# A two-layer decoder trunk: the tile pools of SBUF put at other places of a partition

## The chip, the core and the metric

The kernel runs on one core of a Trainium2 chip. The metric is the device time of that core in microseconds (us), from the first to the last instruction of one launch with what lies around it. Three runs of the kernel before took 659.36, 659.92 and 660.2 us; their median, 659.92 us, is the time before.

## The reference

A residual stream x of 256 tokens by 1024 columns, in fp32, goes through two layers, each a mixer and a gated feed-forward network (FFN), with an RMS norm ahead of each:

```python
for layer in range(2):
    h = rmsnorm(x, norm_mix[layer])
    if layer % 2 == 0:            # even: indexed sparse attention (8 heads, top 64 keys)
        y = h @ ev_w_in           #       beside differential attention (4 heads)
        mix = concat([dsa_mixer(...), diff_mixer(...)]) @ ev_w_out
    else:                         # odd: compressed, selected and window attention (16 heads)
        y = h @ od_w_in
        mix = nsa_mixer(...) @ od_w_out
    x = x + mix
    x = x + (silu(h2 @ w_gate) * (h2 @ w_up)) @ w_down     # h2 = rmsnorm(x, norm_ffn[layer]), 2816 wide
return rmsnorm(x, norm_final)
```

All weights are fp32 and each is used once, 107 MB in all.

## The kernel before

**Numbers.** To keep fp32 accuracy with TensorE's faster fp32r format, every weight tile and every activation is split into a high part (rounded to fp32r) and a low part (the rest). A product is then three matmuls: high by high, high by low, low by high. The helper `mm3` issues these three; its lines are L330, L331 and L332 of the profile. In the FFN's gate and up projections one matmul of 512 columns takes the high weight by both parts of the activation (L437), and one of 256 columns the low weight by the high part (L438).

**Weights.** `Weights` streams tiles of 128 partitions by 4096 bytes from HBM. `load` (L95) issues the DMA on SyncE's queue into one of four raw buffers (`w_raw`), now and then into the buffer of the norm's gain; `prepare` makes the high part on ScalarE (L110) into one of seven `w_hi` buffers and the low part on VectorE (L113) into one of seven `w_lo` buffers. Preparation runs six tiles ahead of use.

**Stages.** Per layer: input projection, attention, output projection, gate and up, down projection. In a projection into the mixer (`project`) the activation `aW` is the stationary operand (128 columns, loaded by LDWEIGHTS) and the weight is the moving operand of 512 columns or fewer, into `ps_in`. The output projection and the FFN's down projection are one function, `residual`: the stationary operand is the attention's output `aT` (`oT` in the code), or the FFN's hidden activation `hT_hi`/`hT_lo`; the moving operand is the weight, in two halves of 512 columns; four accumulators `ps_out` are used in turn. In gate and up the weight is stationary and `aW` moving, into `ps_g` and `ps_u`. Transposes through TensorE have the data as the stationary operand and an identity matrix, the first 128 columns of the constants `con`, as the moving one.

**Order.** A scheduling layer sets the order of each engine from data dependences, and semaphores between the engines; places marked with `keep_in_program_order` (`pin`) hold theirs. Buffers of one tag are used in rotation, so a write to a buffer waits for the readers of what was there.

**Where the buffers lie.** Each tile pool is a stretch of the 229,376 bytes of a partition. Within a pool the tiles follow each other in the order in which their tags first appear, each padded to a multiple of 32 bytes. Before, all pools grow from the low end: `base` (x, constants), `wpool` (raw, high and low weights), `acts` (small activations, and `aW` among them), and behind them the pool of the present stage (`even`, `ffn` or `odd`), which is given back when the stage ends.

Of the kernel before, what the change touches and what calls it, by code (L numbers as in the profile page):

```python
# [7 lines left out]
F32 = mybir.dt.float32  # L8
F32R = mybir.dt.float32r
# [7 lines left out]
T = 256  # L17
P = 128
NT = T // P
KD = D // P  # L20
# [11 lines left out]
WCOLS = 1024  # L32
# [6 lines left out]
def ff_kk(w):  # L39
    return WCOLS // w  # L40


def layer_tiles(chunks):
    tiles = in_tiles(chunks) + [(1, D)] * KD
    for w in FF_CHUNKS:
        tiles += [(ff_kk(w), w)] * (2 * KD // ff_kk(w))
    return tiles + [(1, D)] * KF
# [27 lines left out]
class Weights:  # L75


    def __init__(self, tc, pool, flats, specs, ahead, bufs, spare):
        self.tc, self.pool, self.ahead, self.bufs, self.spare = tc, pool, ahead, bufs, spare
        self.queue = []  # L80
        for flat, tiles in zip(flats, specs):
            off = 0
            for kk, w in tiles:
                n = kk * w
                self.queue.append((flat[off : off + P * n].rearrange("(p c) -> p c", p=P), kk, w))
                off += P * n
        self.raw = []
        self.ready = []
        self.used = 0

    def load(self, upto):
        while len(self.raw) < min(upto, len(self.queue)):
            src, kk, w = self.queue[len(self.raw)]
            raw = self.spare(len(self.raw)) or self.pool.tile([P, WCOLS], F32, tag="raw", bufs=self.bufs[0], name="w_raw")
            self.tc.keep_in_program_order(self.tc.nc.sync.dma_start(raw[:, : kk * w], src))  # L95
            self.raw.append(raw)

# [27 lines left out]
def trunk(tc, x, w0, w1, sm0, cw, vec, gcol, cst, out, dbg=None):  # L125
# [3 lines left out]
    from contextlib import ExitStack  # L129

    ctx = ExitStack()
    base = ctx.enter_context(tc.tile_pool(name="base", bufs=1))
    wpool = ctx.enter_context(tc.tile_pool(name="wpool", bufs=1))
    ap = ctx.enter_context(tc.tile_pool(name="acts", bufs=1))
    psum = ctx.enter_context(tc.tile_pool(name="psum", bufs=1, space=PSUM))

    def mm_bank(name):
        return psum.tile([P, 512], F32, tag="mm", bufs=4, name=name)

    def s_bank(name):  # L140
        return psum.tile([P, 512], F32, tag="s", bufs=2, name=name)

    def t_bank(name):
        return psum.tile([P, 512], F32, tag="tp", bufs=2, name=name)

    def nat(name):
        return ap.tile([P, 512], F32, tag="nat", bufs=4, name=name)


    tiles = [layer_tiles(EV_CHUNKS), layer_tiles(OD_CHUNKS)]  # L150
# [7 lines left out]
            return ap.tile([P, D], F32, tag="gain", bufs=1, name="w_raw")  # L158
        return None

    W = Weights(tc, wpool, [w0, w1], tiles, ahead=6, bufs=(4, 7), spare=spare)
    xs = [base.tile([P, D], F32, tag=f"x{t}", name=f"x{t}") for t in range(NT)]
    con = base.tile([P, C_END], F32, tag="con", name="con")
    small = base.tile([P, V_END - V_KV], F32, tag="small", name="small")
# [8 lines left out]
    def gain(off):  # L173
        new_gain(off)
        tc.keep_in_program_order(load_gain(off, nc.sync))
# [17 lines left out]
    def load_x(t, h):  # L193
        c = slice(512 * h, 512 * h + 512)
        pin(nc.sync.dma_start(xs[t][:, c], x[t * P : (t + 1) * P, c]))

    load_x(0, 0)
    W.load(1)
    load_x(1, 0)
    W.load(2)  # L200
    load_x(0, 1)
    load_x(1, 1)
    W.load(4)
    pin(nc.sync.dma_start(con[:, P:], cst[:, P:]))
# [10 lines left out]
    def evac(dst, src):  # L215
        A.activation(dst, src, AF.Copy)
# [10 lines left out]
    def small_tile(n, tag, bufs=4):  # L227
        return ap.tile([P, n], F32, tag=tag, bufs=bufs, name=tag)
# [4 lines left out]

    def new_wide():

        w = ap.tile([P, KD, 2, T], F32R, tag="aW", name="aW")
        return w, [[w[:, :, z, t * P : (t + 1) * P] for z in range(2)] for t in range(NT)]

    def split(hi, lo, src):
        A.activation(hi, src, AF.Copy)  # L240
        V.tensor_sub(lo, src, hi)  # L241
# [10 lines left out]
    class Norm:  # L252


        def __init__(self, goff):
            self.goff = goff
            self.wide, self.aT = new_wide()
            self.rs = [small_tile(1, "rs") for _ in range(NT)]
            self.last = None
            self.ms = [None] * NT  # L260
# [73 lines left out]
    def project(aT, w, nm=None):  # L334
# [4 lines left out]
        for g in range(n):  # L339
            wh, wl = W.next()  # L340
            for i in range(kk):
# [6 lines left out]
    def residual(act, nk, tail, nxt, rs=None, amid=None):  # L348
# [3 lines left out]
        def one(t, h, k, wt):  # L352
            c = slice(512 * h, 512 * h + 512)
            mm3(ps[t][h], act[t], k, wt[0][:, 0, c], wt[1][:, 0, c], k == 0, k == nk - 1)

        for k in range(nk - tail):
            wt = W.next()
            for t in range(NT):
                for h in range(2):
                    one(t, h, k, wt)  # L360
        last = [W.next(hold=tail) for _ in range(tail)]
        if amid:
# [39 lines left out]
    def ffn(nm, goff):  # L402
        wide, rs = nm.wide, nm.rs
        gain(goff)
        nxt = Final() if goff == V_FIN else Norm(goff)
        with tc.tile_pool(name="ffn", bufs=1, reuse_waits="tile") as fp:
            hh = fp.tile([P, KF, T], F32R, tag="hh", name="hT_hi")
            hl = fp.tile([P, KF, T], F32R, tag="hl", name="hT_lo")


            ones = fp.tile([P, P], F32, tag="ones", name="ones")
            G.memset(ones, 1.0)
            rB = fp.tile([P, T], F32, tag="rB", name="rB")

            def spread():
                dg = nat("dg")
                pb = t_bank("ps_r")
                for t in range(NT):
                    c = slice(t * P, (t + 1) * P)
                    V.tensor_scalar(dg[:, c], ident, rs[t], None, op0=ALU.mult)  # L420
                    TE.matmul(pb[:, c], ones, dg[:, c], start=True, stop=True)
                evac(rB, pb[:, :T])

            f0 = 0
            for w in FF_CHUNKS:
                kk = ff_kk(w)
                nf = w // P
                gp = [mm_bank("ps_g") for _ in range(nf)]
                up = [s_bank("ps_u") for _ in range(nf)]
                for dst in (gp, up):  # L430
                    for g in range(KD // kk):
                        wh, wl = W.next()
                        for i in range(kk):
                            k = g * kk + i
                            for f in range(nf):
                                c = slice(f * P, (f + 1) * P)
                                TE.matmul(dst[f], wh[:, i, c], wide[:, k].rearrange("p z q -> p (z q)"), start=k == 0, stop=False)  # L437
                                TE.matmul(dst[f][:, :T], wl[:, i, c], wide[:, k, 0], start=False, stop=k == KD - 1)  # L438
                        nm.finish()
                    if dst is gp and f0 == 0:  # L440
                        spread()
                for f in range(nf):
                    sg = fp.tile([P, T], F32, tag="sg", bufs=3, name="sg")
                    hn = fp.tile([P, T], F32, tag="hn", bufs=3, name="hn")
                    evac(sg, gp[f][:, T:])
                    V.tensor_add(sg, gp[f][:, :T], sg)
                    V.tensor_mul(sg, sg, rB)
                    A.activation(sg, sg, AF.Silu)
                    evac(hn, up[f][:, T:])
                    V.tensor_add(hn, up[f][:, :T], hn)  # L450
                    V.tensor_mul(hn, hn, sg)
                    split(hh[:, f0 + f], hl[:, f0 + f], hn)
                f0 += nf
            hT = [[z[:, :, t * P : (t + 1) * P] for z in (hh, hl)] for t in range(NT)]
            residual(hT, KF, 3, nxt, rs)
        return nxt


    def even_mixer(nm, goff):
        aT, rs = nm.aT, nm.rs  # L460
        with tc.tile_pool(name="even", bufs=1, reuse_waits="tile") as pool:

            def early(name):
                return pool.tile([P, D], F32, tag="aT", bufs=2 * NT, name=name)
# [248 lines left out]

    def odd_mixer(nm, goff):
        aT, rs = nm.aT, nm.rs
        with tc.tile_pool(name="odd", bufs=1, reuse_waits="tile") as pool:

            def early(name):
                return pool.tile([P, D], F32, tag="aT", bufs=2 * NT, name=name)
# [227 lines left out]
    for t in range(NT):  # L947
        for h in range(2):
            first.square(t, h)
    n = even_mixer(first, V_FFN0)  # L950
    n = ffn(n, V_MIX1)
    n = odd_mixer(n, V_FFN1)
    ffn(n, V_FIN)
    ctx.close()

# [129 lines left out]
```

## Time and profile before

| what | value |
|---|---|
| median of three runs | 659.92 us |
| span of the profiled execution | 658.3 us (no other time of that execution is listed; the median lies 1.6 us above the span) |
| TensorE matmul busy | 644.6 us (98%) |
| VectorE, ScalarE, GpSimd busy | 488.3, 396.6, 12.9 us (74%, 60%, 2%) |
| mean granted TensorE clock | 0.996 |
| DMA | 109.15 MB, 166 GB/s over the span |
| gate and up of the first layer, of the second | 139 to 263 us, 467 to 590 us |
| down projection of the first layer, of the second | 263 to 325 us, 590 to 651 us |

Times are from the start of the span. Busy shares are of the span. Matmuls are pipelined and the profile models their ends, so a matmul's listed duration is longer than the distance to the next; where it matters, distances between starts are read instead. The chain of waits follows the last instruction back to what released it, at each step.

### The profile page before, as it was taken

The page shows a single profiled execution, that of the slowest core. Times are in us where ns is not written, and L with a number is a line of the kernel's source. Part 1 is how long each engine was busy: PE and PEld are TensorE (multiplying, and loading weights), DVE is VectorE, ACT ScalarE, POOL GpSimd, SP SyncE. Part 2 cuts the span into 40 slices and gives each one's busy share as a digit, 9 for nine tenths or more (in the row PEclk, how much of TensorE's full clock was granted, in tenths as well). Part 3 has the DMA queues.
Part 4 walks back from the last instruction along what each step waited for, and adds up shares of the span by engine and source line. Part 5 has one row for each costly group of instructions (what it writes and reads, how often), then busy time and mean ns, then how long its engine had stood idle before and what let it go on. Part 6 is the DMA issues. An engine that isn't in the chain of part 4 may idle for free.

```text
span 658.3 us, 10005 instructions
## 1 busy us (share of the span) xinstructions
PE 644.6 (98%) x3512; PEld 535.8 (81%) x3512; DVE 488.3 (74%) x1115; ACT 396.6 (60%) x800; POOL 12.9 (2%) x26
## 2 busy tenths in 40 slices
PE   8999999999999999999999999999999999999995
PEld 5978888788888888888888877776888888888884
DVE  5999977758978787543579889796698787875424
ACT  6786758548755555433377599696586555554312
POOL 2000000000000000000000000000000000000000
PEclk8999999999999999999999999999999999999999
DMA  8844354038866666663098312420486666665501
GB/s 295 298 132 150 97 183 139 32 133 260 249 194 190 193 188 191 192 190 112 25 372 279 126 39 97 160 65 1 159 270 212 192 191 192 193 192 186 189 10 65
DMA packets 31729, 109.15 MB, mean 166 GB/s; under 512 B 3648, under 2 KB 3904, under 8 KB 31424
## 3 DMA queue, kind: packets, MB, share of 16 engines
q1 hardware_dynamic: 31104, 107.92, 51.2%
q8 instruction: 28, 0.46, 0.3%
q10 hardware_dynamic: 576, 0.59, 0.3%
q14 instruction: 21, 0.17, 0.1%
HBM read 107.46 MB, written 1.05 MB: 165 GB/s over the span
## 4 chain that ended last, share of the span: by engine, by line
PE 85%; ACT 5%; DVE 4%; DMA 3%; issue 2%; POOL 0%; SPq 0%; POOLq 0%; ACTq 0%
PE ps_u L437 12%; PE ps_g L437 11%; PE ps_out L330 7%; PE ps_out L332 7%; PE ps_out L331 7%; PE ps_u L438 6%; PE ps_g L438 6%; PE ps_in L330 5%; PE ps_in L331 5%; PE ps_in L332 5%; DMA w_raw<-in_w 3%; PE ps_o L934 2%; PE pt_p L918 2%; PE ps_s L899 2%; ACT w_hi L110 1%
## 5 line engine op out<-in xcount | busy, mean ns | idle before, releaser
L113 DVE TENSOR_TENSOR w_lo<-w_raw,w_hi 128x1024 fp32r<-128x1024 f32 (+5 forms) x200 | 234.9, 1182 | 95.1 <-ACT w_hi L110 92.9
L110 ACT ACTIVATE w_hi<-w_raw 128x1024 fp32r<-128x1024 f32 (+5 forms) x200 | 203.3, 1022 | 133.2 <-PE ps_out L332 59.6
L437 PE MATMUL ps_u<-aW,w_hi 128*128 128x512 f32 x352 | 123.4, 394 | 0.4 <-DVE hn L450 0.4
L437 PE MATMUL ps_g<-aW,w_hi 128*128 128x512 f32 x352 | 123.4, 394 | 0.3 <-DVE aW L241 0.3
L438 PE MATMUL ps_g<-aW,w_lo 128*128 128x256 f32 x352 | 97.6, 277 | 0.0
L438 PE MATMUL ps_u<-aW,w_lo 128*128 128x256 f32 x352 | 97.6, 277 | 0.0
L437 PEld LDWEIGHTS ps_g<-aW,w_hi 128*128 128x128 f32 x352 | 66.0, 187 | 16.2 <-DVE aW L241 0.9
L437 PEld LDWEIGHTS ps_u<-aW,w_hi 128*128 128x128 f32 x352 | 66.0, 188 | 15.9 <-DVE hn L450 0.7
L330 PE MATMUL ps_in<-w_hi,aW 128*128 128x512 f32 (+5 forms) x208 | 77.3, 372 | 0.6 <-ACT aW L240 0.6
L331 PE MATMUL ps_in<-w_lo,aW 128*128 128x512 f32 (+5 forms) x208 | 77.4, 372 | 0.1
L332 PE MATMUL ps_in<-w_hi,aW 128*128 128x512 f32 (+5 forms) x208 | 75.6, 364 | 0.0
L332 PE MATMUL ps_out<-w_hi,hT_lo 128*128 128x512 f32 x176 | 69.4, 395 | 0.0
L331 PE MATMUL ps_out<-w_lo,hT_hi 128*128 128x512 f32 x176 | 69.4, 395 | 0.0
L330 PE MATMUL ps_out<-w_hi,hT_hi 128*128 128x512 f32 x176 | 69.4, 395 | 0.0
L438 PEld LDWEIGHTS ps_g<-aW,w_lo 128*128 128x128 f32 x352 | 66.1, 188 | 0.0
L438 PEld LDWEIGHTS ps_u<-aW,w_lo 128*128 128x128 f32 x352 | 66.1, 188 | 0.0
L400 ACT ACTIVATE e<-e,bias 128x128 f32<-128x128 f32 (+1 forms) x96 | 42.4, 446 | 2.4 <-DVE bias L399 2.4
L330 PEld LDWEIGHTS ps_in<-w_hi,aW 128*128 128x128 f32 x208 | 39.5, 190 | 5.3 <-ACT aW L240 0.8
L331 PEld LDWEIGHTS ps_in<-w_lo,aW 128*128 128x128 f32 x208 | 39.5, 190 | 4.4 <-issue 0.5
L332 PEld LDWEIGHTS ps_in<-w_hi,aW 128*128 128x128 f32 x208 | 39.4, 189 | 4.4 <-issue 0.5
L332 PEld LDWEIGHTS ps_out<-w_hi,hT_lo 128*128 128x128 f32 x176 | 32.9, 187 | 8.1
L330 PEld LDWEIGHTS ps_out<-w_hi,hT_hi 128*128 128x128 f32 x176 | 32.9, 187 | 8.0
(225 smaller groups left out, 888.1 us busy)
## 6 DMA issues: line engine op xcount, KB each, us to landing
w_raw<-in_w SPq DMA_DIRECT2D x176, 512.0 KB, 4.3
w_raw<-in_w SPq DMA_DIRECT2D x8, 384.0 KB, 4.5
gain<-in_vec SPq DMA_DIRECT2D x4, 512.0 KB, 4.4
cw<-in_cw SPq DMA_DIRECT2D x2, 1024.0 KB, 7.7
w_raw<-in_w SPq DMA_DIRECT2D x4, 416.0 KB, 5.2
w_raw<-in_w SPq DMA_DIRECT2D x4, 328.0 KB, 5.2
w_raw<-in_w SPq DMA_DIRECT2D x4, 304.0 KB, 2.9
x<-in_x SPq DMA_DIRECT2D x4, 256.0 KB, 5.2
```

What stands on the lines that cost most here:

```text
L110: act = nc.scalar.activation(hi[:, :n], raw[:, :n], AF.Copy)
L113: nc.vector.tensor_sub(lo[:, :n], raw[:, :n], hi[:, :n])
L330: TE.matmul(ps, act[0][:, k], wh, start=start, stop=False)
L331: TE.matmul(ps, act[0][:, k], wl, start=False, stop=False)
L332: TE.matmul(ps, act[1][:, k], wh, start=False, stop=stop)
L400: A.activation(e, e, AF.Exp, scale=-1.0, bias=bias, accum_out=den)
L437: TE.matmul(dst[f], wh[:, i, c], wide[:, k].rearrange("p z q -> p (z q)"), start=k == 0, stop=False)
L438: TE.matmul(dst[f][:, :T], wl[:, i, c], wide[:, k, 0], start=False, stop=k == KD - 1)
L899: mmi = TE.matmul(sb[:, i], qS[t][:, h], kz[:, par, :, :ns], start=z == 0, stop=z == 1)
L918: TE.transpose(pt[:, i, b, st], e[:, i, b, st * P : (st + 1) * P], ident)
L934: pin(TE.matmul(ob[64 * par : 64 * par + 64], vv[:, st, c : c + 64], pTs[par][:, b, st].rearrange("p j c -> p (j c)"), start=False, stop=l ...
```

## The change

The pools are put on two sides. From the low end now grow `wpool` with the high and low weights only, a new pool `widep` with `aW` alone, and the stage's pool. From the high end grow `base`, a new pool `rpool` with the raw weights, and `acts`. No size, tag, rotation or instruction differs: each engine's list is the same in the same order, and every instruction waits for the same semaphore counts. The addresses in the built program, in bytes of a partition:

| buffer | bytes | start before | start now |
|---|---|---|---|
| x, two halves | 2 x 4096 | 16512 | 214752 |
| constants `con` | 4264 | 24704 | 222944 |
| `w_raw` | 4 x 4096 | 31104 | 198368 |
| `w_hi` | 7 x 4096 | 47488 | 16512 |
| `w_lo` | 7 x 4096 | 76160 | 45184 |
| `aW` | 16384 | 106880 | 73856 |
| `nat` (x times gain, rope and others) | 4 x 2048 | 123392 | 184608 |
| gain | 4096 | 131712 | 192928 |
| `hT_hi` | 22528 | 137152 | 90240 |
| `hT_lo` | 22528 | 159680 | 112768 |
| attention's output `aT`, even layer | 4 x 4096 | 137152 | 90240 |
| attention's output `aT`, odd layer | 4 x 4096 | 143040 | 96128 |

So TensorE's operands lie 31 to 47 thousand bytes lower, except the identity in `con`, x, and what is transposed out of `nat`, which lie higher.

```diff
 class Weights:
-    def __init__(self, tc, pool, flats, specs, ahead, bufs, spare):
-        self.tc, self.pool, self.ahead, self.bufs, self.spare = tc, pool, ahead, bufs, spare
+    def __init__(self, tc, pool, rpool, flats, specs, ahead, bufs, spare):
+        self.tc, self.pool, self.rpool, self.ahead, self.bufs, self.spare = tc, pool, rpool, ahead, bufs, spare
...
-            raw = self.spare(len(self.raw)) or self.pool.tile([P, WCOLS], F32, tag="raw", bufs=self.bufs[0], name="w_raw")
+            raw = self.spare(len(self.raw)) or self.rpool.tile([P, WCOLS], F32, tag="raw", bufs=self.bufs[0], name="w_raw")
...
-    base = ctx.enter_context(tc.tile_pool(name="base", bufs=1))
-    wpool = ctx.enter_context(tc.tile_pool(name="wpool", bufs=1))
-    ap = ctx.enter_context(tc.tile_pool(name="acts", bufs=1))
+    base = ctx.enter_context(tc.tile_pool(name="base", bufs=1, side="right"))
+    rpool = ctx.enter_context(tc.tile_pool(name="rpool", bufs=1, side="right"))
+    ap = ctx.enter_context(tc.tile_pool(name="acts", bufs=1, side="right"))
+    wpool = ctx.enter_context(tc.tile_pool(name="wpool", bufs=1, side="left"))
+    wide_pool = ctx.enter_context(tc.tile_pool(name="widep", bufs=1, side="left"))
...
-        w = ap.tile([P, KD, 2, T], F32R, tag="aW", name="aW")
+        w = wide_pool.tile([P, KD, 2, T], F32R, tag="aW", name="aW")
...
-        with tc.tile_pool(name="ffn", bufs=1, reuse_waits="tile") as fp:
+        with tc.tile_pool(name="ffn", bufs=1, side="left", reuse_waits="tile") as fp:
...
-        with tc.tile_pool(name="even", bufs=1, reuse_waits="tile") as pool:
+        with tc.tile_pool(name="even", bufs=1, side="left", reuse_waits="tile") as pool:
...
-        with tc.tile_pool(name="odd", bufs=1, reuse_waits="tile") as pool:
+        with tc.tile_pool(name="odd", bufs=1, side="left", reuse_waits="tile") as pool:
```

More of the change, by code (lines that the diff above doesn't have):

```diff
@@ L159, in spare @@
         return None
-    W = Weights(tc, wpool, [w0, w1], tiles, ahead=6, bufs=(4, 7), spare=spare)
+    W = Weights(tc, wpool, rpool, [w0, w1], tiles, ahead=6, bufs=(4, 7), spare=spare)
     xs = [base.tile([P, D], F32, tag=f"x{t}", name=f"x{t}") for t in range(NT)]
```

## The prediction

> **What bounds the kernel now.** I read the page first: the engines' busy time, the granted clock, and the chain of waits.
>
> ```profile
> PE 644.6 (98%) x3512; PEld 535.8 (81%) x3512; DVE 488.3 (74%) x1115; ACT 396.6 (60%) x800; POOL 12.9 (2%) x26
> PEclk8999999999999999999999999999999999999999
> PE 85%; ACT 5%; DVE 4%; DMA 3%; issue 2%; POOL 0%; SPq 0%; POOLq 0%; ACTq 0%
> PE ps_u L437 12%; PE ps_g L437 11%; PE ps_out L330 7%; PE ps_out L332 7%; PE ps_out L331 7%; PE ps_u L438 6%; PE ps_g L438 6%; PE ps_in L330 5%; PE ps_in L331 5%; PE ps_in L332 5%; DMA w_raw<-in_w 3%; PE ps_o L934 2%; PE pt_p L918 2%; PE ps_s L899 2%; ACT w_hi L110 1%
> ```
>
> TensorE is the bound: 85% of the chain that ended last is its matmuls, and the granted clock is full from the second slice on. The first projection's and the softmaxes' ACT and DVE steps and a few weight transfers make up the rest. Nothing in the change alters an instruction, a wait or an order, so the time can move only if the duration of an instruction depends on where its operands lie. The question is whether the trace of before shows such a dependence. The listed duration of a matmul is modelled, so I looked at the distance from one start to the next, stage by stage, for matmuls of 512 columns that follow each other without a gap. The columns of the timeline are start, duration, engine, line, operands and shape.
>
> ```profile
> 349.19 0.39 PE L332 MATMUL ps_in<-w_hi,aW 128*128 128x512 f32 x1
> ...
> 351.91 0.39 PE L332 MATMUL ps_in<-w_hi,aW 128*128 128x512 f32 x1
> ```
> ```profile
> 289.94 0.39 PE L332 MATMUL ps_out<-w_hi,hT_lo 128*128 128x512 f32 x1
> ...
> 292.04 0.39 PE L332 MATMUL ps_out<-w_hi,hT_lo 128*128 128x512 f32 x1
> ```
> ```profile
> 131.70 0.39 PE L330 MATMUL ps_out<-w_hi,aT 128*128 128x512 f32 x1
> ...
> 134.96 0.39 PE L332 MATMUL ps_out<-w_hi,aT 128*128 128x512 f32 x1
> ```
>
> Between the two rows of the odd layer's input projection lie 12 steps: 2.72 / 12 = 226.7 ns each. Between those of the FFN's down projection lie 9 steps: 2.10 / 9 = 233.3 ns. Between those of the even layer's output projection lie 14 steps: 3.26 / 14 = 232.9 ns. All three are the same three instructions of `mm3` with a moving operand of 512 columns out of the same weight buffers. They differ in where the stationary operand lies: in `aW` (106880 to 123264) in the first, behind 137152 in the other two. The longer distance is no accident of one place; it holds through the whole stage, whatever VectorE, ScalarE and the DMA do at the time:
>
> ```profile
> core 0: us, PE busy (x) PEld busy (x) DVE busy (x) ACT busy (x) POOL busy (x), PEclk, DMA share, GB/s
> 160.00:255.00 95.00, 95.00 (x550) 83.08 (x549) 77.91 (x127) 59.05 (x109) 0.00 (x0) 1.00 0.69 202
> 265.00:305.00 40.00, 40.00 (x173) 32.08 (x172) 18.89 (x19) 15.12 (x15) 0.00 (x0) 1.00 0.60 178
> 595.00:640.00 45.00, 45.00 (x195) 36.06 (x194) 17.57 (x16) 14.81 (x14) 0.00 (x0) 1.00 0.41 129
> ```
>
> A window counts up to two matmuls that began before it. So 40 us hold about 171.5 down-projection matmuls and 45 us about 193: 233 ns each in both layers. Gate and up (first row) hold about 274 pairs of one 512-column and one 256-column matmul: 346.7 ns a pair, or 0.4514 ns a column. Were every step its columns at one rate r plus one fixed part f, the projection gives 512 r + f = 226.7 and the pair 768 r + 2 f = 346.7; so 256 r = 106.7, r = 0.4167 ns and f = 13.3 ns. Gate and up thus pay the same 13.3 ns per matmul as the input projections; with the same r the down projection pays 233.3 - 213.3 = 20.0 ns. That is an extra of 6.7 ns per matmul in exactly the stages whose stationary operand lies in the stage's pool.
>
> **What is different about that pool.** Two things about the addresses. First, height: the slow stationary operands lie above 131072 bytes while the weights that stream meanwhile lie below; in the fast stages both lie below. Second, an offset: divided by 128, `w_hi`, `w_lo` and `aW` (47488, 76160, 106880) leave nothing, but `hT_hi`, `hT_lo` and both layers' `aT` (137152, 159680, 143040) leave 64, and the steps inside are multiples of 512 bytes. Neither alone suffices. In the odd layer's scores both operands lie in the pool, above 179904, and both leave 64; in that layer's first projection (304 columns) the second half of a weight tile starts at 1216 bytes, so there the moving operand leaves 64 and the stationary one nothing, both below 131072:
>
> ```profile
> 381.68 0.28 PE L899 MATMUL ps_s<-kX,qS 128*128 128x256 f32 x1
> ...
> 381.92 0.28 PE L899 MATMUL ps_s<-kX,qS 128*128 128x256 f32 x1
> ```
> ```profile
> 328.30 0.30 PE L330 MATMUL ps_in<-w_hi,aW 128*128 128x304 f32 x1
> ...
> 328.99 0.30 PE L332 MATMUL ps_in<-w_hi,aW 128*128 128x304 f32 x1
> ```
>
> Two steps in 0.24 us, 120 ns each, less 256 r = 106.7: 13.3 ns. Five steps in 0.69 us, 138 ns each, less 304 r = 126.7: 11 ns. Neither pays 20. What is left by addresses is a stationary operand above 131072 with a moving one below, or a stationary one at 64 with a moving one at 0. Height as a slope is out: the window of 265 to 305 us walks 15 KB up `hT_hi` and `hT_lo` each, 22528 bytes apart, at one rate. Now `w_hi`, `w_lo`, `aW`, `hT_hi`, `hT_lo` and both layers' `aT` (16512, 45184, 73856, 90240, 112768, 96128) all leave nothing, and only the last 4224 bytes of `hT_lo` lie above 131072. Under both readings the extra goes.
>
> **The sum.** How many matmuls pay the extra:
>
> ```profile
> L332 PE MATMUL ps_out<-w_hi,hT_lo 128*128 128x512 f32 x176 | 69.4, 395 | 0.0
> L331 PE MATMUL ps_out<-w_lo,hT_hi 128*128 128x512 f32 x176 | 69.4, 395 | 0.0
> L330 PE MATMUL ps_out<-w_hi,hT_hi 128*128 128x512 f32 x176 | 69.4, 395 | 0.0
> L330 PE MATMUL ps_out<-w_hi,aT 128*128 128x512 f32 x64 | 26.8, 418 | 0.1
> L331 PE MATMUL ps_out<-w_lo,aT 128*128 128x512 f32 x64 | 26.1, 407 | 0.0
> L332 PE MATMUL ps_out<-w_hi,aT 128*128 128x512 f32 x64 | 26.0, 411 | 0.0
> ```
>
> That is 528 in the down projections and 192 in the output projections, 720 in all; 720 x 6.67 ns = 4.8 us if each step shortens the span. The down projections surely count in full: 528 x 6.67 = 3.5 us, as the windows above show TensorE without a gap. Part of the output projections is filler while ScalarE and VectorE work through the attention. The chain says how much: its three ps_out rows, 7% each, are some 145 us (three times 7 to 7.5% of the span, 138 to 148); by 233 ns that is 622 matmuls (592 to 635), 4.1 us. I take 4.1 us. Bounds: 4.8 above; below, 3.5 less 0.2 if height decides (four of 22 steps of `hT_lo`, 33 matmuls in both layers), so 3.3.
>
> What follows a down projection comes earlier by the same amount, since it starts from its end: `gain`, small DMAs and weights wait on SyncE's queue for the readers of the old pool, and the chain runs from ps_out through the transposes into them.
>
> **What the other moved buffers cost.** Transposes now read an identity that leaves 96 on division by 128 and, out of `nat`, data that leave 32. Before they read remainder 0 for the identity against 0 (`xg` in `nat`) or 64 (`stk` in the odd pool):
>
> ```profile
> 320.20 0.44 PE pt_a L247 x4
> 360.71 0.87 PE pt_q L827 x8
> ```
>
> 0.44 / 4 = 110 ns and 0.87 / 8 = 109 ns: the offset costs a transpose nothing, since a stationary load each sets their pace. I take 0. Bounds: 0, and 6.67 ns for each of the 319 transposes in the program, 2.1 us, if remainder 32 were worse than 64.
>
> Other matmuls of the attentions have both operands in the pool and keep their distance; 0.
>
> VectorE and ScalarE now read raw weights, x, gain and `nat` at remainders 32 and 96. Before, only 0 and 64 occur for wide operands:
>
> ```profile
> L447 DVE TENSOR_TENSOR sg<-sg,rB 128x256 f32<-128x256 f32 x44 | 18.7, 425 | 1.2
> L395 DVE TENSOR_TENSOR nk<-nk,rope_b 128x256 f32<-128x256 f32 x4 | 1.7, 419 | 0.0
> L271 DVE TENSOR_TENSOR xg<-x,gain 128x512 f32<-128x512 f32 x12 | 8.2, 688 | 0.2
> L395 DVE TENSOR_TENSOR nq<-nq,rope_b 128x512 f32<-128x512 f32 x4 | 2.8, 691 | 0.0
> L113 DVE TENSOR_TENSOR w_lo<-w_raw,w_hi 128x1024 fp32r<-128x1024 f32 x176 | 214.3, 1224 | 81.0 <-ACT w_hi L110 78.8
> ```
>
> The first has both inputs at 64, the second at 0 and 64; the third all at 0, the fourth at 0 and 64: 425 against 419 and 688 against 691 ns. No dependence of VectorE within 1.5%; I take 0. What hides a small one: L113's 81 us of idle time before it in gate, up and down projection. Bound: VectorE's and ScalarE's 9% of the chain, 59 us; 1.5% of that is 0.9 us. The raw weights' DMAs write rows of up to 4096 bytes, now to remainder 96; their 3% of the chain, 20 us, would give 0.4 us for 2%. I take 0.
>
> Sum against the profiled execution: 658.3 - 4.1 = 654.2 us of span. The median of the runs lies 1.6 us above the span, so the time is 659.9 - 4.1 = **655.8 us**, a gain of 0.6%.
>
> The Trainium skill speaks against a gain. Its page "TensorE: Matmul & The Clock Gate", under "Step-by-step: what each phase is for", gives TensorE two independent SBUF read ports, so that "Loading the next tile's weights doesn't steal SBUF read bandwidth from the running matmul", and its "Back-to-back issue gap" gives a 512-column step as 512/2.4 + 2.5 = 216 ns with no term for an address. The trace does not agree with the figure: 226.7 and 233.3 ns above. By that rule the sum would be 0; it is the first rival below.
>
> **Rivals.**
>
> 1. *No change, 659.9 us.* The 6.7 ns come from the code of `residual` (four accumulators in turn, where a projection uses two), not from addresses. For it: every slow stage is that function, so the trace cannot part the two. And the two readings by address each needed a second condition. Against it: the instructions and shapes are those of a projection, and gate and up, with yet another order of accumulators, pay 13.3 ns as the projections do.
>
> 2. *Slower, 661.7 us.* Remainders 32 and 96 stretch VectorE's and ScalarE's instructions on raw weights, x and `nat`. Place: the softmax and norm chains and the weight preparation ahead of them, 59 us of the chain. Price: 10% longer is 5.9 us, less 4.1 is 1.8 slower. It decides from 4.1 / 59 = 7% on. Against it: nothing from 0 to 64 in the rows above. For it: no row has 32.
>
> 3. *A larger gain, 649.6 us.* The 13.3 ns that remain depend on position as well, and fall with operands 31 to 47 thousand bytes lower. A third of it, 4.4 ns, over the 1408 matmuls of gate and up alone is 6.2 us on top of 4.1, so 649.6; half as much gives 652.7. Against it: `w_hi`, `w_lo` and `aW` span 76 thousand bytes before, and projections and gate and up pay the same 13.3 although they exchange which of them is stationary.
>
> **How the numbers follow.** Forecast: 0.60. Rival 1: 0.24. Rival 2: 0.08. Rival 3: 0.08. The forecast's own range is a gain of 4.8 to one of 3.3 less 1.3 (0.9 and 0.4 above): 655.1 to 657.9 us; with the transposes' 2.1 it ends at rival 1. The range takes in rival 1 and rival 3 down to half its price: 652.7 to 660.2, which leaves out some 0.12, and what I have not thought of. A run of this kernel differs by 0.1% from the next; I call 0.2%, 1.3 us, the bound of no change. Faster: forecast and rival 3, 0.68; same: 0.24; slower: 0.08.
>
> **What will show it.** If right, the distance between down-projection matmuls falls from 233.3 to 226.7 ns, the 40 us that held 171.5 of them hold 176.5, and that stage is 1.8 us shorter in each layer; input projections stay at 226.7 and gate and up at 346.7 a pair; L113, L447 and L271 keep 1224, 425 and 688 ns. If the height decides, the last four steps of `hT_lo` in each down projection stay long. It is wrong if the 233.3 stay (rival 1), if VectorE's and ScalarE's means rise while ps_out gets shorter (rival 2), or if gate and up change (rival 3).

## The result, and the profile after

The kernel after takes 658.26 us (median of 8 runs, 656.45 to 659.6), the kernel before, run beside it, 661.68 us (8 runs, 659.36 to 664.64). The ratio is 0.9946, with a 95% interval of 0.9922 to 0.997: faster by 0.5%. The prediction was 655.8 us, a ratio of 0.9938 to its base of 659.92 us. The gain came out nearly as forecast, 0.54% for 0.62%: 3.4 us, inside the forecast's own 2.0 to 4.8. The absolute time is 2.5 us above the forecast; it lies 0.4 us above the forecast's own range (655.1 to 657.9) and inside the whole one, mostly because the three runs shown of before had been low ones (659.92 us, where the eight beside the kernel after have 661.68).

The execution profiled took 659.6 us, with a span of 657.8 us. From its page, busy time and the chain of waits (lines of the code are two higher than before, from the added pools on):

```profile
PE 643.6 (98%) x3512; PEld 538.5 (82%) x3512; DVE 488.4 (74%) x1115; ACT 396.7 (60%) x800; POOL 13.0 (2%) x26
PE 84%; ACT 6%; DVE 4%; DMA 4%; issue 2%; POOL 1%; SPq 0%; POOLq 0%; ACTq 0%
```

TensorE remains the bound. Now the distances between starts, as for before: the down projection of the second layer over 180 steps, its last four matmuls, and the odd layer's input projection over 12 steps. From the timeline of the kernel after (start, duration, engine, line, operands and shape):

```profile
596.12 0.39 PE L334 MATMUL ps_out<-w_hi,hT_lo 128*128 128x512 f32 x1
...
636.92 0.39 PE L334 MATMUL ps_out<-w_hi,hT_lo 128*128 128x512 f32 x1
...
649.84 0.39 PE L334 MATMUL ps_out<-w_hi,hT_lo 128*128 128x512 f32 x1
...
650.52 0.39 PE L334 MATMUL ps_out<-w_hi,hT_lo 128*128 128x512 f32 x1
```
```profile
351.73 0.39 PE L334 MATMUL ps_in<-w_hi,aW 128*128 128x512 f32 x1
...
354.45 0.39 PE L334 MATMUL ps_in<-w_hi,aW 128*128 128x512 f32 x1
```

40.80 / 180 = 226.7 ns a step, where before had 233.3; the last three steps, 0.68 / 3 = 226.7 ns, two that read `hT_hi` and one that reads the part of `hT_lo` above 131072, are no longer than the rest. The input projection keeps 2.72 / 12 = 226.7 ns. But gate and up changed, in the first layer only. First the first layer, then the second, 80 pairs each, from the timeline of after:

```profile
199.87 0.40 PE L439 MATMUL ps_g<-aW,w_hi 128*128 128x512 f32 x1
...
228.14 0.40 PE L439 MATMUL ps_u<-aW,w_hi 128*128 128x512 f32 x1
...
519.80 0.39 PE L439 MATMUL ps_u<-aW,w_hi 128*128 128x512 f32 x1
...
547.53 0.39 PE L439 MATMUL ps_g<-aW,w_hi 128*128 128x512 f32 x1
```

28.27 / 80 = 353.4 ns a pair in the first layer, 27.73 / 80 = 346.6 ns in the second; before had 346.7 in both. A layer has 352 pairs, so this costs 352 x 6.67 ns = 2.35 us of the gain. The boundaries of the stages show all of it: the first matmul of gate and up, of the down projection, of the next layer's input projection and output projection, and so on to the last matmul. From the timelines of before and of after:

```profile
139.05 0.39 PE L437 MATMUL ps_g<-aW,w_hi 128*128 128x512 f32 x1
...
262.87 0.40 PE L330 MATMUL ps_out<-w_hi,hT_hi 128*128 128x512 f32 x1
...
325.80 0.30 PE L330 MATMUL ps_in<-w_hi,aW 128*128 128x304 f32 x1
...
418.44 0.47 PE L330 MATMUL ps_out<-w_hi,aT 128*128 128x512 f32 x1
...
466.70 0.50 PE L437 MATMUL ps_g<-aW,w_hi 128*128 128x512 f32 x1 [0.27 <-DVE aW L241]
...
589.77 0.39 PE L330 MATMUL ps_out<-w_hi,hT_hi 128*128 128x512 f32 x1
...
651.13 0.40 PE L332 MATMUL ps_out<-w_hi,hT_lo 128*128 128x512 f32 x1
```
```profile
139.93 0.39 PE L439 MATMUL ps_g<-aW,w_hi 128*128 128x512 f32 x1
...
265.95 0.40 PE L332 MATMUL ps_out<-w_hi,hT_hi 128*128 128x512 f32 x1
...
327.20 0.30 PE L332 MATMUL ps_in<-w_hi,aW 128*128 128x304 f32 x1
...
419.61 0.48 PE L332 MATMUL ps_out<-w_hi,aT 128*128 128x512 f32 x1
...
467.78 0.50 PE L439 MATMUL ps_g<-aW,w_hi 128*128 128x512 f32 x1 [0.27 <-DVE aW L243]
...
590.86 0.39 PE L332 MATMUL ps_out<-w_hi,hT_hi 128*128 128x512 f32 x1
...
650.52 0.39 PE L334 MATMUL ps_out<-w_hi,hT_lo 128*128 128x512 f32 x1
```

| stretch | before, us | after, us | difference, us |
|---|---|---|---|
| start to gate and up of layer 1 | 139.05 | 139.93 | +0.88 |
| gate and up 1 | 123.82 | 126.02 | +2.20 |
| down projection 1 | 62.93 | 61.25 | -1.68 |
| input projection 2 and attention up to the output projection | 92.64 | 92.41 | -0.23 |
| output projection 2 with the attention around it | 48.26 | 48.17 | -0.09 |
| gate and up 2 | 123.07 | 123.08 | +0.01 |
| down projection 2 | 61.36 | 59.66 | -1.70 |
| rest of the span | 7.17 | 7.28 | +0.11 |
| span | 658.3 | 657.8 | -0.5 |

So these two executions differ by only 0.5 us: the down projections gave 3.4 us, gate and up took 2.2 back, and the start 0.9. The start's 0.9 us arise ahead of the first output projection (105.38 before, 106.33 now): TensorE's first input projection began at 7.0 us before and 7.8 us here, and at 6.8 and 7.1 us in two further profiles of after, so most of this part varies from one execution to the next and is not the change's. Whether the 2.2 us are, is what the experiments had to find, beside what it is in an address that decides.

VectorE kept its durations, from the groups of after, shapes apart (before: 1224, 425 and 688 ns):

```profile
L113 DVE TENSOR_TENSOR w_lo<-w_raw,w_hi 128x1024 fp32r<-128x1024 f32 x176 | 214.0, 1222 | 79.6 <-ACT w_hi L110 77.1
L449 DVE TENSOR_TENSOR sg<-sg,rB 128x256 f32<-128x256 f32 x44 | 18.6, 423 | 1.2
L273 DVE TENSOR_TENSOR xg<-x,gain 128x512 f32<-128x512 f32 x12 | 8.2, 688 | 0.2
```

### The profile page after: what moved, and what is told of

It reads as the page before. It is cut to its first block, busy times and chain, and to the rows that moved or that the text cites. A ratio compares the mean times of both kernels' runs of the same rounds, so it can differ in the third digit from the quotient of the medians.

```text
span 657.8 us, 10005 instructions
## 1 busy us (share of the span) xinstructions
PE 643.6 (98%) x3512; PEld 538.5 (82%) x3512; DVE 488.4 (74%) x1115; ACT 396.7 (60%) x800; POOL 13.0 (2%) x26
## 3 DMA queue, kind: packets, MB, share of 16 engines
q1 hardware_dynamic: 31104, 107.92, 49.6%
## 4 chain that ended last, share of the span: by engine, by line
PE 84%; ACT 6%; DVE 4%; DMA 4%; issue 2%; POOL 1%; SPq 0%; POOLq 0%; ACTq 0%
PE ps_u L439 12%; PE ps_g L439 11%; PE ps_out L332 7%; PE ps_out L334 7%; PE ps_out L333 7%; PE ps_u L440 6%; PE ps_g L440 6%; PE ps_in L332 5%; PE ps_in L334 5%; PE ps_in L333 5%; DMA w_raw<-in_w 2%; PE ps_o L936 2%; PE pt_p L920 2%; ACT w_hi L110 2%; PE ps_s L901 2%
```

## Experiments

All addresses below are of one partition. "Distance" is the address of the activation (`hT`, `aT` or `aW`) less that of the weights (`w_hi`, `w_lo`), modulo 256 bytes; it is the same for every matmul of 512 columns of a stage, since the steps inside the buffers are multiples of 512 bytes there. Before, it is 64 for `hT` and `aT` and 0 for `aW`; after, it is 0 for all three.

**e1: the stationary operand at remainder 0 modulo 128, but still high.** The two readings that the prediction left open part here: height, or remainder 64. Edit to the kernel before; the unused tile moves `hT_hi` and `hT_lo` up by 64 bytes, to 137216 and 159744 (distance 128).

```diff
         with tc.tile_pool(name="ffn", bufs=1, reuse_waits="tile") as fp:
+            pad = fp.tile([P, 16], F32, tag="pad", name="pad")
             hh = fp.tile([P, KF, T], F32R, tag="hh", name="hT_hi")
```

> The kernel before, with 64 unused bytes ahead of the FFN's hidden activation: hT_hi starts at 137216 and hT_lo at 159744, both a multiple of 128 and still above 131072. Nothing else moves but the FFN's own small buffers. If the remainder on 128 decides, the down projections go from 233.3 to 226.7 ns a step in both layers (528 x 6.7 = 3.5 us faster than before), output projections stay at 233. If the height decides, they stay at 233.3 and the time stays. If the step is a state into which a stage falls whatever its addresses, either can come, and not the same in both layers.

Measured: 662.09 us (10 runs, 660.68 to 665.38) against 662.1 us for before, a ratio of 1.0009 [0.9991, 1.0028]. The down projection over 180 steps, and gate and up of the second layer over 80 pairs, from the timeline of e1:

```profile
595.79 0.40 PE L332 MATMUL ps_out<-w_hi,hT_lo 128*128 128x512 f32 x1
...
637.63 0.39 PE L332 MATMUL ps_out<-w_hi,hT_lo 128*128 128x512 f32 x1
```
```profile
519.72 0.40 PE L438 MATMUL ps_g<-aW,w_hi 128*128 128x512 f32 x1
...
547.98 0.40 PE L438 MATMUL ps_u<-aW,w_hi 128*128 128x512 f32 x1
```

41.84 / 180 = 232.4 ns, which is neither 233.3 nor 226.7. Remainder 64 modulo 128 is therefore not the whole rule, and taken alone this looked like height. Gate and up, whose buffers had not moved, stood at 353.3 ns a pair in both layers of this execution (28.26 / 80 here): the 353.3 does not need the pools' new places. It is most of why this profile is long (span 663.6 us): the two stages take 4.4 of the 5.3 us more than in the profile shown of before.

**e2: the stationary operand at remainder 64, but low.** The same unused tile in the kernel after; `hT_hi` and `hT_lo` at 90304 and 112832 (distance 64).

```diff
         with tc.tile_pool(name="ffn", bufs=1, side="left", reuse_waits="tile") as fp:
+            pad = fp.tile([P, 16], F32, tag="pad", name="pad")
             hh = fp.tile([P, KF, T], F32R, tag="hh", name="hT_hi")
```

> The changed kernel, with 64 unused bytes ahead of the FFN's hidden activation: hT_hi at 90304 and hT_lo at 112832, both 64 off a multiple of 128, and below 131072 but for the end. If the remainder decides, down projections return to 233.3 ns a step and the time is 3.5 us above the changed kernel's. If the height decides, they keep 226.9 and the time stays. If it is a state of the stage, either can come.

Measured: 661.23 us (10 runs, 658.96 to 663.37), a ratio to before of 0.9976 [0.9955, 0.9996]. From the timeline of e2, 180 steps:

```profile
595.98 0.39 PE L334 MATMUL ps_out<-w_hi,hT_lo 128*128 128x512 f32 x1
...
637.98 0.39 PE L334 MATMUL ps_out<-w_hi,hT_lo 128*128 128x512 f32 x1
```

42.00 / 180 = 233.3 ns: with every pool where the change put it, 64 bytes bring the whole 6.7 ns back, and the median lies 3.3 us above that of the kernel after on the same chip (657.9, the next entry), where 528 x 6.67 ns = 3.5 us had been expected. Height falls, and so does the first rival (the code of `residual`), which is the same in all of these. Gate and up stood at 353.3 ns a pair in the first layer and 346.7 in the second, as in the kernel after.

**The kernel after again.** The same code, to see which of its numbers repeat.

> The changed kernel once more, for a second profile. In the first its gate and up took 353.3 ns a pair in the first layer and 346.7 in the second (346.7 in both before). If addresses set this, the same comes again, layer by layer. If it is a state that a stage falls into by chance, another combination can come; down projections should keep 226.9 in both layers, as both theories by address say.

Measured: 657.9 us (6 runs, 656.24 to 659.45), a ratio of 0.9931 [0.9905, 0.9958], with the down projection at 227.0 ns (the mean of both layers) and gate and up again at 353.3 ns a pair in the first layer and 346.7 in the second.

**Matmuls alone, at chosen addresses.** This kernel leaves the computation out: it fills one large tile, and issues 36 matmuls a stretch in the patterns of the down projection (`dn`), the input projection (`in`) and gate and up (`gu`), four times over the list, while no weights are fetched from HBM or split.

```diff
+# name, pattern, address of the weights, address of the activations
+CASES = [
+    ("dn_hi_odd", "down", 47488, 137152),
+    ("dn_lo_even", "down", 24704, 90240),
+    ("dn_hi_even", "down", 47488, 137216),
...
+    ("dn_both_odd", "down", 47552, 137152),
+    ("dn_w_odd", "down", 47552, 106880),
...
+    ("gu_act_q", "gate", 47488, 106912),
+]
```

> The matmuls alone: it leaves out the whole computation and runs 80 stretches of 36 matmuls on one filled buffer, 20 cases of addresses four times each, with a pause of differing length ahead of each stretch. dn: order of the down projection (moving 512 columns, four accumulators), in: order of the input projection (two accumulators), gu: gate and up pairs (512 and 256 columns). hi and lo: the stationary operand above or below 131072; odd: 64 off a multiple of 128; q and s: 32 and 16 off; even: a multiple of 128. By remainder: dn_hi_odd, dn_lo_odd and in_hi_odd, in_lo_odd settle at 233.3 ns, dn_hi_even, dn_lo_even, dn_lo_aW, in_lo_even and in_hi_even at 226.7. By height: dn_hi_odd, dn_hi_even and in_hi_odd, in_hi_even at 233.3, the lo cases at 226.7. By the order of residual: all dn at 233.3, all in at 226.7. If a state is fallen into by chance, the four repeats of a case differ. gu_before and gu_after: 346.7 and 353.3 if addresses set gate and up, either in both if chance does.

Measured, from the timeline (start of the stretch, time to its last end, tile, matmuls):

```profile
171.36 6.40 PE L65 MATMUL gu_act_q<-big 128*128 128x512 f32 x36
177.60 8.55 PE L65 MATMUL dn_hi_odd<-big 128*128 128x512 f32 x36
185.99 8.36 PE L65 MATMUL dn_lo_even<-big 128*128 128x512 f32 x36
194.19 8.53 PE L65 MATMUL dn_hi_even<-big 128*128 128x512 f32 x36
...
219.14 8.36 PE L65 MATMUL dn_both_odd<-big 128*128 128x512 f32 x36
227.34 8.41 PE L65 MATMUL dn_w_odd<-big 128*128 128x512 f32 x36
```

A stretch holds its first steps, after the change of pattern, too; the settled steps, the mean from the thirteenth on, are 233.4 ns for `dn_hi_odd` (distance 64), 226.7 for `dn_lo_even` (0), 232.3 for `dn_hi_even` (128), 226.7 for `dn_both_odd` (0) and 229.0 for `dn_w_odd` (192). The four repeats of a case agree within 0.1 ns, but for the very first stretch, which began with steps of 427 ns. `dn_both_odd` decides: its stationary operand lies high and at remainder 64, as before had it, but its weights lie at 64 too, and the 6.7 ns are gone. Neither operand's own place counts, only the distance between the two. The 232.3 of `dn_hi_even` is e1's 232.4 without any DMA or split beside it. Two more stretches, 16 and 32 bytes off, took 233.3 ns. Gate and up took 353.3 ns a pair (settled) in five arrangements (three of them at distance 0) and 346.7 in one: `gu_act_q`, 32 bytes off.

**The scan.** Matmuls alone again (the computation is left out), 48 a stretch, the activation 0 to 480 bytes off the weights in steps of 32; behind them gate-and-up stretches at 0 and at 32 bytes, entered by a first matmul of another width each time.

```diff
+RELS = list(range(0, 512, 32))
+CASES = [(f"in_{r}x", "in", 47488, 106880 + r, 0) for r in RELS]
+CASES += [(f"gu_{r}x", "gate", 47488, 106880 + r, 0) for r in RELS]
+CASES += [(f"gu_0x", "gate", 47488, 106880, 512 - 20 * v) for v in range(1, 9)]
+CASES += [(f"gu_32x", "gate", 47488, 106912, 512 - 20 * v) for v in range(1, 9)]
```

> The matmuls alone again, the whole computation left out: 96 stretches of 48. The new theory: the settled step depends on the distance between stationary and moving operand modulo 512 bytes, not on the remainder of one of them, nor on height. in_0x to in_480x: input-projection order, activations (stationary) 0 to 480 bytes off the weights modulo 512. Expected 226.7 ns at 0, 233.3 at 32 and 64, 232.3 at 128, 229.0 at 448, 233.3 at 480, as far as the first scan showed them. gu_0x to gu_480x: gate and up order with the same offsets, weights stationary; expected 353.3 a pair at 0 and 64, 346.7 at 32. Sixteen more stretches of gu_0x and gu_32x begin with a matmul of another width, so that the pairs start at another phase: if gate and up at offset 0 have two states, some of them settle at 346.7; at 32 all do.

Measured, from the timeline (a row is one run of matmuls that lie in the window asked for: start, time to its last end, count):

```profile
478.77 6.51 PE L48 MATMUL in_0x<-big 128*128 128x512 f32 x28
...
490.68 6.70 PE L48 MATMUL in_32x<-big 128*128 128x512 f32 x28
...
501.65 6.70 PE L48 MATMUL in_64x<-big 128*128 128x512 f32 x28
...
546.38 6.80 PE L48 MATMUL in_192x<-big 128*128 128x512 f32 x29
...
568.75 6.51 PE L48 MATMUL in_256x<-big 128*128 128x512 f32 x28
```

Less the last matmul's 0.39 us, 27 steps of `in_0x` take 6.12 us, 226.7 ns each; those of `in_32x` and `in_64x` 6.31, 233.7 (a hundredth of a microsecond is 0.4 ns here); 28 of `in_192x` 6.41, 228.9; and `in_256x` is `in_0x` again. The settled values of all stretches, in ns, were the same for N and N + 256:

| distance, bytes | 0 | 32 | 64 | 96 | 128 | 160 | 192 | 224 |
|---|---|---|---|---|---|---|---|---|
| 512-column step, activation stationary | 226.7 | 233.4 | 233.4 | 234.3 | 232.4 | 233.4 | 228.8 | 233.3 |
| gate/up pair, weights stationary | 353.3 or 346.7 | 346.7 | 353.3 | 350.0 | 351.1 | 346.7 | 353.3 | 353.3 |

At distance 0, gate and up showed two rates: of 16 entries behind a matmul of another width 12 settled at 353.3 ns and 4 at 346.7; without such a matmul all four (0 and 256) settled at 353.3. At 32 all 16 settled at 346.7. The other distances were entered in one way only, four times each, so a second rate there is not excluded. The period is 256 bytes; of what was seen, 0 is best for the projections, 32 or 160 for gate and up.

**The kernel before again.**

> The kernel before once more, for a second profile. In the first both layers' gate and up took 346.7 ns a pair; the later profiles of both layouts had 353.3 in the first layer or in both. If that is a state which a stage falls into, one or both layers come at 353.3 here, 352 pairs x 6.7 ns = 2.3 us a layer; down and output projections stay at 233.3, as their offset says.

Measured: 660.19 us, span 658.4 us. The down projection stood at 233.3 ns. Gate and up began the first layer slowly and became faster within it; windows of 10 us of this kernel (after each engine's busy time, in brackets, its instructions):

```profile
145.00:155.00 10.00, 10.00 (x59) 8.68 (x58) 7.32 (x10) 7.19 (x9) 0.00 (x0) 1.00 0.82 295
165.00:175.00 10.00, 10.00 (x60) 8.81 (x59) 8.99 (x18) 7.33 (x15) 0.00 (x0) 1.00 0.80 245
```

59 matmuls in 10 us, then 60; by starts 353.3 ns a pair up to 157 us, and 346.7 from 158 us to the stage's end. The change falls on a wait of TensorE:

```profile
157.34 0.28 PE L438 MATMUL ps_g<-aW,w_lo 128*128 128x256 f32 x1
157.90 0.50 PE L437 MATMUL ps_u<-aW,w_hi 128*128 128x512 f32 x1 [0.28 <-DVE hn L450]
```

The same wait turned the other way in e2: 346.7 ns a pair before it (at 157 us there), 353.3 after it. In none of the 22 gate-and-up stages profiled did the settled rate change but at an interruption of the stream of pairs (a wait, or transposes in between). So one stage can go from one rate to the other with nothing changed in the program, the rate is taken up anew behind an interruption, and the kernel before has both rates as well.

**e3: gate and up at distance 32.** If distance 0 has two rates, the change's time can be bettered. In the kernel after, the FFN's `aW` starts 32 bytes into a tile that is 32 bytes longer; unused tiles of 224 bytes at the head of the three stage pools bring `hT` and `aT` back to distance 0. In the odd stage their room comes from one small buffer (`hk`, 256 bytes), put into the place of a later one.

```diff
-    def new_wide():
+    def new_wide(off=0):
-        w = wide_pool.tile([P, KD, 2, T], F32R, tag="aW", name="aW")
+        w = wide_pool.tile([P, KD * 2 * T + 8], F32R, tag="aW", name="aW"); w = w[:, off : off + KD * 2 * T].rearrange("p (k z t) -> p k z t", k=KD, z=2)
...
-            self.wide, self.aT = new_wide()
+            self.wide, self.aT = new_wide(8 if goff in (V_FFN0, V_FFN1) else 0)
...
-            hh = fp.tile([P, KF, T], F32R, tag="hh", name="hT_hi")
+            pad = fp.tile([P, 56], F32, tag="pad", name="pad"); hh = fp.tile([P, KF, T], F32R, tag="hh", name="hT_hi")
...
-                hk = pool.tile([P, 64], F32, tag="hk", name="hk")
+                hk = pool.tile([P, T], F32, tag="cT", bufs=1, name="hk")[:, :64]
```

> The kernel after, with the activation of gate and up 32 bytes off the weights modulo 256 in both layers, and every other distance as in the kernel after (a pad of 224 bytes keeps hT and aT at 0). Theory (the distance between the two operands modulo 256 bytes sets the step, and at distance 0 gate and up have two states): gate and up take 346.7 ns a pair in both layers and in every run; down projection 226.7 ns a step; the time is about 2.3 us (one layer's 352 pairs by 6.67 ns) below that of the kernel after in a run whose first layer had 353.3, so 654 to 656 us, and the runs lie closer together than those of the kernel after. Rival (the 353.3 comes from something else in the run, such as the DMAs or the temperature of the chip): gate and up still show 353.3 ns in one layer in some runs, and the time is that of the kernel after, about 658 us.

Measured: 657.34 us (6 runs, 655.71 to 658.3), a ratio to before of 0.9913 [0.9888, 0.9938]; 654 to 656 us had been expected. From the timeline of e3, gate and up over 80 pairs in both layers:

```profile
199.88 0.39 PE L439 MATMUL ps_g<-aW,w_hi 128*128 128x512 f32 x1
...
227.61 0.39 PE L439 MATMUL ps_u<-aW,w_hi 128*128 128x512 f32 x1
...
519.86 0.39 PE L439 MATMUL ps_u<-aW,w_hi 128*128 128x512 f32 x1
...
547.59 0.39 PE L439 MATMUL ps_g<-aW,w_hi 128*128 128x512 f32 x1
```

27.73 / 80 = 346.6 ns in both, and the down projection kept 226.7. The gain over the kernel after is 1.5 us beside the runs of the next entry, less than the 2.3 expected of a run with one slow layer. Some runs of after may have had none, but no profiled one shows that.

**The kernel after a third time**, on the chip of e3.

> The kernel after again, on the same chip as the two beside it, as the measure for them: a ratio of 0.993 to 0.995 to the kernel before, down projection 226.7 ns, gate and up 346.7 or 353.3 ns a pair by run and layer. If gate and up stand at 346.7 in both layers in the profiled run, that run should lie about 2.3 us below one with 353.3 in the first layer.

Measured: 658.87 us (10 runs, 657.24 to 660.37), a ratio of 0.9941 [0.9921, 0.996]. Gate and up: 353.3 ns a pair in the first layer, 346.7 in the second, for the third time.

**e4: the kernel before with 192 bytes of unused tile.** `hT` goes to distance 0 and stays above 131072, `aT` stays at 64; no pool is moved.

```diff
-            hh = fp.tile([P, KF, T], F32R, tag="hh", name="hT_hi")
+            pad = fp.tile([P, 48], F32, tag="pad", name="pad"); hh = fp.tile([P, KF, T], F32R, tag="hh", name="hT_hi")
```

> The kernel before, with an unused tile of 192 bytes ahead of hT_hi, so that hT_hi and hT_lo lie at distance 0 from the weights modulo 256, above 131072, and no pool is moved to the other end; aT stays at distance 64. Theory: down projection 226.7 ns a step instead of 233.3, so 528 x 6.67 = 3.5 us below the kernel before, a ratio of about 0.995, with the same scatter from gate and up; the move to the other end was not needed for this part. Rival (height decides, or remainder 64 of the stationary operand alone): as the stationary operand now leaves 0 modulo 128 but lies above 131072, height would keep 233.3 ns and a ratio of 1.000; the remainder alone would give 226.7, but e1, which had remainder 0 as well, has already shown 232.4 at distance 128.

Measured: 659.82 us (12 runs, 656.97 to 662.66), a ratio of 0.9953 [0.993, 0.9975]: 2.5 us less than before, where 3.5 had been expected, which lies within the interval. From the timeline of e4, the down projection, then gate and up of both layers:

```profile
596.16 0.39 PE L332 MATMUL ps_out<-w_hi,hT_lo 128*128 128x512 f32 x1
...
636.96 0.39 PE L332 MATMUL ps_out<-w_hi,hT_lo 128*128 128x512 f32 x1
```
```profile
199.86 0.39 PE L437 MATMUL ps_g<-aW,w_hi 128*128 128x512 f32 x1
...
227.60 0.39 PE L437 MATMUL ps_u<-aW,w_hi 128*128 128x512 f32 x1
...
519.96 0.40 PE L437 MATMUL ps_u<-aW,w_hi 128*128 128x512 f32 x1
...
548.23 0.40 PE L437 MATMUL ps_g<-aW,w_hi 128*128 128x512 f32 x1
```

40.80 / 180 = 226.7 ns: the down projections' gain without the move. In this execution it was the second layer whose gate and up ran at 353.4 ns (28.27 / 80) and the first at 346.8.

**e5: the kernel before with all the distances of e3**, by unused tiles of 160 bytes in the stage pools and the same edits to `aW` and `hk`; no pool is moved.

```diff
-        w = ap.tile([P, KD, 2, T], F32R, tag="aW", name="aW")
+        w = ap.tile([P, KD * 2 * T + 8], F32R, tag="aW", name="aW"); w = w[:, off : off + KD * 2 * T].rearrange("p (k z t) -> p k z t", k=KD, z=2)
...
-            hh = fp.tile([P, KF, T], F32R, tag="hh", name="hT_hi")
+            pad = fp.tile([P, 40], F32, tag="pad", name="pad"); hh = fp.tile([P, KF, T], F32R, tag="hh", name="hT_hi")
```

> The kernel before, no pool moved to the other end, but small unused tiles set the same distances as in e3: hT and aT at 0 from the weights modulo 256, the activation of gate and up at 32. If the distances are all that the change altered: the time of e3, 656 to 658 us (ratio 0.991), down projection 226.7 ns, output projections 230 ns with their edges, gate and up 346.7 ns a pair in both layers. If something else in the move saved or cost time (raw weights, x and gain at remainders 32 and 96, operands lower): the down and gate steps are the same, but the time differs from e3's by more than its interval.

Measured: 657.03 us (6 runs, 656.03 to 657.64), a ratio of 0.9919 [0.9896, 0.9942]; the down projection settled at 226.7 ns, gate and up at 346.7 a pair in both layers.

**e3 again**, on the chip of e5.

> The kernel e3 again, on the same chip as e5: 656 to 658 us, ratio 0.991, gate and up 346.7 ns a pair in both layers. Should a layer show 353.3 ns, distance 32 does not fix the state and the theory of the two states at distance 0 falls.

Measured: 657.3 us (6 runs, 656.8 to 657.69), a ratio of 0.9925 [0.99, 0.9949]; gate and up settled at 346.7 ns in both layers once more. The medians of e5 and e3 agree within 0.3 us, so beyond the distances nothing of the move shows, as far as their intervals (some 0.25% either way) can tell. Both are better than the two kernels given. Over all runs e3 has a median of 657.3 us (12 runs, 655.71 to 658.3), the kernel after 658.4 (24 runs, 656.24 to 660.37), a ratio of 0.998.

## Why the prediction was right, and where not

- **The term of the sum held.** 6.67 ns off each matmul of the down projections: predicted 233.3 to 226.7, measured 226.7, 1.68 and 1.70 us a layer where 1.8 was said. Input projections (226.7 ns), VectorE's groups and transposes (109 ns from one to the next in both kernels) kept their durations, as the terms of 0 had it.
- **The address reading was not settled, and neither of the two left open is right.** The extra does not go by one operand's place: height is refuted by e2 and e4 (233.3 low, 226.7 high), remainder 64 of the stationary operand by e1 (232.4 at remainder 0) and by `dn_both_odd` (226.7 at remainder 64). It goes by the distance modulo 256. Of the two rows that made the prediction ask for a "second condition", one is the distance itself: both operands of `ps_s<-kX,qS` lie, by the sizes of the tiles ahead of them, from 204480 and 179904 on and leave 192 modulo 256, so their distance is 0. The other is not explained: the second half of the 304-column tile lies at distance 64 (106880 - 48704 = 58176, 64 above a multiple of 256), yet its steps take 138 ns, as do those of the first half at distance 0 (six in 0.83 us from 325.80 us on, in the profile shown of before). So the rule is shown for steps of 512 columns and for the pairs of gate and up, not for narrower steps. That both readings gave the right number is luck: the change happens to bring all of these stages to distance 0. The remainder would have been wrong for e1, the height for e2 and e4.
- **Gate and up were taken as fixed at 346.7 ns a pair.** That step failed. At distance 0, before and after alike, they have two rates, and the profile shown of before had the fast one in both layers, those of after the slow one in the first layer. So the sum was made against a lucky execution. This cost 2.2 us of the profile after, but not of the verdict, as other executions of before's gate and up are slow too (the first 18 us of the second profile of before, both layers of e1, the second layer of e4, all with the same addresses there): the medians differ by 661.68 - 658.26 = 3.4 us, about what the down projections gave. Whether the change also alters which rate is taken is not shown. With the pools of after and distance 0, all four profiled executions (e2's too) ended the first layer slow and the second fast; with the pools of before (e1's and e4's too), one of four first layers and two of four second layers ended slow.
- **The 0.6 us for output projections was too much.** Their steps did fall, from 234 to 230 ns in the mean over matmuls that follow each other, those at a change of tile included, but the stretch with the second layer's got shorter by 0.09 us and the first layer's by about 0.07 (33.67 to 33.60 us). The rest, it seems, lies beside ScalarE's and VectorE's attention work; no run parts it. To read a number of path matmuls off three rounded shares of the chain was the weak step: even the lower bound, 592, leaves 64 matmuls beside the 528 of the down projections, where the 0.16 us are worth 24. A printed 7% can also stand for 6.5%, which the bound left out: three times that is 128 us, or 550 matmuls.
- **The spread.** "A run differs by 0.1% from the next" rested on three runs; the 63 runs of before timed here reach from 659.36 to 665.6 us, 0.9%. With gate and up fixed at their fast rate, the runs of e3 and e5 keep within 0.4%. That the rest of before's spread is gate and up's two rates (0, 1 or 2 layers at 2.35 us) fits, but only profiled executions show the rate, so it is argued for the others.
- **The rivals.** No change (structure) is refuted by e2 and e4; slower (VectorE on remainders 32 and 96) by 1222 against 1224 ns; of the larger gain, "gate and up change" was right as a place, though with the other sign in the profile after, and e3 is the version of it that pays; its mechanism, lower operands, was not, as e5 has the same time with no pool moved.
- The Trainium skill, page "TensorE: Matmul & The Clock Gate", section "Back-to-back issue gap", has 512/2.4 + 2.5 = 216 ns for a 512-column step, which it calls the gap of an isolated matmul, and about 131 ns for one in a stream with weight loads; neither has a term for an address. The runs show 226.7 to 234.3 by distance alone. The prediction was right to go by the rows.

## What to carry to other kernels

Where TensorE bounds a kernel and each matmul loads new weights, read the distance between starts stage by stage and compare stages of equal shape; a difference of 3% between them may, with 512 columns, come from nothing but the distance of the two operands' addresses modulo 256 bytes, and an unused tile of at most 224 bytes sets it. Before a profile serves as the base of a sum, look at whether it is a typical execution: the median of more runs, and a second profile, would have shown gate and up's second rate. A change that moves buffers is also a change of every such distance, so list these ahead of any other effect.

## What was not expected of the hardware

- A 512-column fp32r step with a new stationary operand takes 226.7 ns at distance 0 and up to 234.3 ns at other multiples of 32 bytes, with a period of 256 bytes. The absolute place of either operand made no difference in any run here.
- With the weights stationary and moving operands of 512 and 256 columns in turn, distance 0 has two settled rates, 346.7 and 353.3 ns a pair, taken up at the entry to the stage or behind an interruption within it; distances 32 and 160 showed only 346.7, the latter in four entries.
- Why 256 bytes, why 304 columns at distance 64 pay nothing, and what chooses between the two rates, is open: the runs vary addresses and entries, and show nothing of what lies between the buffers and the array.
